# A decoder block of attention, linear attention and SwiGLU on one core: weight sums on VectorE, six early blocks, form loads on GpSimd's queue

## The chip, the core and the metric

One core of a Trainium2 chip runs the whole kernel in one launch. The metric is the device time of one execution in microseconds (us). The kernel before takes 2258.38 us (median of 3 runs, 2248.99 to 2261.52). Engines: TensorE (PE; PEld are its weight loads), VectorE (DVE), ScalarE (ACT), GpSimd (POOL) and SyncE (SP), which here only issues transfers. GpSimd issues transfers too, in the same queue as its own operations.

## The reference

One block of a transformer with 512 tokens and 2048 features, in float32. The first half mixes tokens by eight heads of softmax attention with low-rank queries and keys, and by four heads of gated linear attention (GLA); the second is a gated feed-forward network (FFN) of width 5632. Each half is normed before and after, and modulated by columns worked out from a vector `c`.

```python
ada = jax.nn.silu(c) @ w_ada[l] + b_ada[l]
shift_m, scale_m, gate_m, shift_f, scale_f, gate_f = [
    t[:, None, :] for t in jnp.split(ada, N_MOD, axis=-1)]
h = rms_norm(x, g_pre_mix[l]) * (1.0 + scale_m) + shift_m
z = h @ w_in[l]
...
o = jnp.concatenate([o_mla, o_gla], axis=-1) @ w_out[l]
x = x + gate_m * rms_norm(o, g_post_mix[l])
h = rms_norm(x, g_pre_ffn[l]) * (1.0 + scale_f) + shift_f
f = (jax.nn.silu(h @ w_ffn_gate[l]) * (h @ w_ffn_up[l])) @ w_ffn_down[l]
x = x + gate_f * rms_norm(f, g_post_ffn[l])
```

## The kernel before

A float32 product is made of three products of halves: each operand is split into a high part (a cast to a narrower format on ScalarE) and a low part (a subtraction on VectorE), and `mm3` (L213) multiplies high by high, high by low and low by high (L214 to L216). Weights arrive by SyncE's queue in pieces of 1 MB (a `wr` tile, four buffers) and are split by `load_split` (L203 is the low part) or, in the FFN, by `wparts` (L904 high, L905 low, into eight `wh` buffers).

The program is written down in an order, and a scheduler with a cost table of its own then sets the order of each engine's instructions; within an engine they run in that order. Small activations are `t2` tiles of 128 by 512, 73 in all.

Ahead of the FFN: `ada` (L228) makes one modulation column from a 1 MB weight piece by a product and a sum on VectorE. 96 columns are needed; the last 64 come from the generator `more`, a few at each step of the fillers, which are pieces of projection work (`fill_qk`, `fill_vr`, `fill_out`) that stand between the attention's steps. `lowrank` (L429) norms the low-rank queries and keys at the same time as the first fillers run.

`out_group` makes the output projection (16 tiles of sums, multiplied by a gain on GpSimd, L887), and `second_norm` (L793) adds the residual, norms each token tile, and multiplies it into `y` (L811, VectorE), which TensorE transposes (L814) and ScalarE scales into `h2` (L820).

The FFN multiplies in seven products in place of eight (the Winograd form of Strassen's scheme). Its activation operands are the forms a11, a12, a22 and s1 to s4, made by `first_forms` (from the first two token tiles) and `more_forms` (needing all four); `parts` splits them (L831 high, L832 low), `minus` is L836. Its weight operands are sums of the four quarters of the weights, made one into the next. `vadd` (L925) adds on VectorE, `padd` (L922) on GpSimd.

There are 22 blocks of 256 columns. The products q1 and q2 need only a11 and a12 and plain weights; for the first `PRO` = 2 blocks they are made early, among the steps of the second norm (the generator `norms`, moved on by `advance`), so that those blocks have five products left in the up loop and the other 20 have seven. Each product of the up loop is two times 24 `mm3`-parts of 256 columns. The results q1 and sg (a silu of a sum of q1 and q2) of an early block stay in `t2` tiles. After every second block `pair_forms` makes the seven forms of the result for the down loop, splits them and stores them to device memory (`spill_parts`, L949, GpSimd's queue). The down loop (five column groups `c_`, two halves `p` each) takes the forms back with `back` (L1025, SyncE's queue), makes seven products a half, and adds each to an accumulator on VectorE. The last two blocks are multiplied plainly at the end: `gate_rows` (L256, L257, L260) fetches gain rows through GpSimd's queue, `gl` fetches the last spilled tiles, the low parts of the last weights are made on GpSimd (L1084), and each sum is added (L1099), squared (L1101) and multiplied by its gain (L1102, GpSimd) before the closing norm.

## Time and profile before

| What | Value |
|---|---|
| Median of 3 runs | 2258.38 us |
| The profiled execution | 2255.43 us |
| Its span on the core | 2253.7 us |
| TensorE busy | 2109.3 us, 94% |
| VectorE busy | 1764.0 us, 78% |
| ScalarE busy | 907.7 us, 40% |
| GpSimd busy | 540.4 us, 24% |
| Mean granted TensorE clock | 0.972 |

Busy time adds up what an engine spends on instructions, with the time that an instruction stands for access to memory within it. TensorE's clock is granted at 2.4 GHz (1.0) or at 1.2 (0.5); a stretch's figure is the mean. A wait is put down to the instruction that released it last. The stages by time: up to 575 us the projections and both kinds of attention, to 767 the output projection, to 900 the second norm with the early blocks, to 1756 the up loop, to 2184.8 the down loop, then the last two blocks and the closing norm.

### The profile page before, as it was taken

To read this page: it belongs to the slowest core of one execution; us is meant where nothing else is said; L and a number is where in the kernel's file an instruction comes from. 1 tells how busy PE (TensorE), PEld (TensorE's weight loads), DVE (VectorE), ACT (ScalarE), POOL (GpSimd) and SP (SyncE) were. 2 spreads that over 40 slices of the span, in tenths; PEclk is the share of its full clock that TensorE was granted. 3 is DMA by queue.
4 is the path that set the end of the run, shared out by engine and by line. 5 is a ranking of instruction groups with operands and counts; after the bars stand their busy time and mean duration, and the time that the engine had idled before them with its cause. 6 is when DMAs were issued, how large, how long until landed. Compare 5 with 4: busy or idle time off the path is not lost. (4 is left out here: it accounts for less than half of the span.)

```text
span 2253.7 us, 32197 instructions
## 1 busy us (share of the span) xinstructions
PE 2109.3 (94%) x12714; PEld 1851.7 (82%) x12714; DVE 1764.0 (78%) x2095; ACT 907.7 (40%) x1265; POOL 540.4 (24%) x436
## 2 busy tenths in 40 slices
PE   7999999996999967999999999999999799999977
PEld 5888777773888867999999999999999687777866
DVE  6885787886475778888888888887887669888984
ACT  5433222324233664444434434434444353333332
POOL 0000000000212332323333333333332232131136
PEclk9999999996999979999999999999999999999989
DMA  8882586885575742434434424433433647564334
GB/s 333 317 306 100 210 306 246 316 311 199 187 247 202 260 178 75 178 133 158 160 122 149 173 113 146 178 113 141 178 128 125 244 178 273 213 217 148 128 131 150
DMA packets 91578, 432.18 MB, mean 192 GB/s; under 512 B 12168, under 2 KB 12280, under 8 KB 54817
## 3 DMA queue, kind: packets, MB, share of 16 engines
q1 hardware_dynamic: 69840, 360.09, 44.0%
q0 software_dynamic: 21584, 70.02, 8.1%
q8 instruction: 100, 1.64, 0.3%
q14 instruction: 52, 0.43, 0.1%
q10 hardware_dynamic: 2, 0.01, 0.0%
HBM read 370.80 MB, written 59.26 MB: 191 GB/s over the span
## 5 line engine op out<-in xcount | busy, mean ns | idle before, releaser
L905 DVE TENSOR_TENSOR wh<-wr,wh 128x1024 fp32r<-128x1024 f32 x448 | 677.8, 1524 | 214.7 <-ACT wh L904 210.3
L904 ACT CAST wh<-wr 128x1024 fp32r<-128x1024 f32 x448 | 464.6, 1050 | 649.0 <-PE ps L215 247.1
L214 PE MATMUL ps<-t,wh 128*128 128x256 f32 x2464 | 705.1, 286 | 18.8 <-ACT wh L904 9.0
L216 PE MATMUL ps<-t,wh 128*128 128x256 f32 x2464 | 704.9, 286 | 12.1 <-DVE wh L905 11.9
L215 PE MATMUL ps<-t,wh 128*128 128x256 f32 x2464 | 703.6, 286 | 4.4 <-DVE t L832 4.4
L214 PEld LDWEIGHTS ps<-t,wh 128*128 128x128 f32 x2464 | 479.0, 194 | 22.5 <-ACT wh L904 11.4
L216 PEld LDWEIGHTS ps<-t,wh 128*128 128x128 f32 x2464 | 478.7, 194 | 15.5 <-DVE wh L905 15.2
L215 PEld LDWEIGHTS ps<-t,wh 128*128 128x128 f32 x2464 | 479.0, 194 | 5.8 <-DVE t L832 5.7
L922 POOL TENSOR_TENSOR wr<-wr 128x1024 f32<-128x1024 f32 x88 | 223.5, 2540 | 500.5 <-DVE wh L905 232.1
L228 DVE CUSTOM_DVE_ANT_0 wr<-wr,cB 128x2048 f32<-128x2048 f32 x96 | 219.2, 2285 | 41.1 <-DMA wr<-w_ada 41.0
L215 PE MATMUL ps<-wh,t 128*128 128x512 f32 x560 | 222.9, 398 | 22.1 <-DVE wh L905 22.1
L214 PE MATMUL ps<-wh,t 128*128 128x512 f32 x560 | 221.4, 396 | 11.4 <-DMA t<-gd 11.3
L216 PE MATMUL ps<-wh,t 128*128 128x512 f32 x560 | 219.9, 395 | 0.5 <-DMA t<-gd 0.5
L202 ACT CAST hi<-wr 128x1024 fp32r<-128x1024 f32 (+3 forms) x122 | 122.7, 1010 | 223.1 <-PE ps L215 134.1
L203 DVE TENSOR_TENSOR lo<-wr,hi 128x1024 fp32r<-128x1024 f32 (+3 forms) x122 | 145.1, 1193 | 67.0 <-ACT hi L202 66.5
L215 PE MATMUL ps<-t,hi 128*128 128x512 f32 x432 | 173.0, 400 | 3.1 <-DVE t L302 3.0
L922 POOL TENSOR_TENSOR wr<-wr,wr 128x2048 f32<-128x2048 f32 x20 | 102.6, 5129 | 303.1 <-DVE wh L905 198.7
L216 PE MATMUL ps<-t,lo 128*128 128x512 f32 x432 | 170.4, 395 | 0.0
L214 PE MATMUL ps<-t,hi 128*128 128x512 f32 x432 | 168.7, 398 | 1.3 <-ACT t L300 1.3
L214 PE MATMUL ps<-hi,t 128*128 128x512 f32 x400 | 161.4, 404 | 1.0 <-DVE t L209 0.9
L925 DVE TENSOR_TENSOR wr<-wr,wr 128x1024 f32<-128x1024 f32 (+1 forms) x108 | 153.3, 1420 | 5.5 <-DMA wr<-w_fu 3.2
L215 PE MATMUL ps<-lo,t 128*128 128x512 f32 x400 | 156.6, 392 | 0.3 <-DVE lo L203 0.3
(230 smaller groups left out, 2656.6 us busy)
## 6 DMA issues: line engine op xcount, KB each, us to landing
wr<-w_ada SPq DMA_DIRECT2D x96, 1024.0 KB, 5.8
wr<-w_fg SPq DMA_DIRECT2D x48, 1024.0 KB, 5.0
wr<-w_fu SPq DMA_DIRECT2D x44, 1024.0 KB, 7.2
wr<-w_fd SPq DMA_DIRECT2D x40, 1024.0 KB, 4.9
gd<-t POOLq DMA_DIRECT2D x148, 256.0 KB, 2.6
t<-gd SPq DMA_DIRECT2D x148, 256.0 KB, 5.3
wr<-w_kqvr SPq DMA_DIRECT2D x24, 1024.0 KB, 4.9
wr<-w_out SPq DMA_DIRECT2D x22, 1024.0 KB, 5.5
```

Of the source, the lines that this page charges most:

```text
L202: A.copy(out=hi[:, :n], in_=r)
L203: V.tensor_tensor(out=lo[:, :n], in0=r, in1=hi[:, :n], op=ALU.subtract)
L214: T.matmul(ps, lhsT=a, rhs=c_, start=start, stop=False)
L215: T.matmul(ps, lhsT=a, rhs=d_, start=False, stop=False)
L216: T.matmul(ps, lhsT=b, rhs=c_, start=False, stop=stop)
L228: V.tensor_tensor_reduce(out=raw, in0=raw, in1=cB, scale=1.0, scalar=0.0, op0=ALU.mult, op1=ALU.add, accum_out=adac[:, j:j + 1])
L904: A.copy(out=hi, in_=src)
L905: V.tensor_tensor(out=lo, in0=src, in1=hi, op=ALU.subtract)
L922: nc.gpsimd.tensor_tensor(out=out, in0=a, in1=b, op=ALU.add)
L925: V.tensor_tensor(out=out, in0=a, in1=b, op=ALU.add)
```

## The change

- Every sum of FFN weights is made by `vadd` on VectorE; `padd` is gone. The gain products L887 and L1102 and the low parts L1084 go from GpSimd to VectorE as well, and `y` (L811) from VectorE to ScalarE.
- `PRO` is 6: six blocks have q1 and q2 made beside the second norm, and `advance` moves it two steps on after each half product, in all of them.
- Sixteen modulation columns go into `fill_qk`, four before each of its four pieces; `fill_vr` has three instead of four at each of 12 steps, and `fill_out` one or two instead of two. They are 64 as before.
- `back` loads spilled forms by GpSimd's queue.

```diff
--- before.py
+++ after.py
@@ -28,7 +28,7 @@
 MAGIC = 12582912.0
 N_T2 = 73
 NBLK = DFF // 256
-PRO = 2
+PRO = 6
 ATT_SCALE = 192.0 ** -0.5
 GLA_SCALE = 128.0 ** -0.5
 
@@ -454,6 +454,8 @@
             pss = [bank("A") for _ in range(4)]
             for kq in (2, 3):
                 w = load_split(w_kqvr[half, kq], 4, 512)
+                for _ in range(4):
+                    next(more)
                 for k, b in ORDER[kq == 3]:
                     mm3(pss[b], cut(w[k], b * P, P), hT[4 * kq + k], kq + k == 2, kq + k == 6)
                 if kq == 3:
@@ -467,7 +469,7 @@
             k0 = 2 if ci < 2 else 0
             for kq in range(k0, 4):
                 w = load_split(w_kqvr[2 + ci, kq], 4, 512)
-                for _ in range(4):
+                for _ in range(3):
                     next(more)
                 for k, b in ORDER[kq == 3]:
                     first, last = kq == k0 and k == 0, kq + k == 6
@@ -499,7 +501,7 @@
             w = ahead
             if i < 7:
                 ahead = load_split(w_out[todo[i + 1]], 4, 512)
-            for _ in range(2):
+            for _ in range(1 + q):
                 next(more)
             if q == 0:
                 pss = [bank("A") for _ in range(NT)]
@@ -808,7 +810,7 @@
         yield
         for n in range(4):
             y = t2()
-            V.tensor_scalar(y, og[t][n], v2, None, op0=ALU.mult)
+            A.activation(y, og[t][n], AF.Copy, scale=v2)
             ps = bank("B")
             for k in range(4):
                 T.transpose(ps[:, k * P:(k + 1) * P], y[:, k * P:(k + 1) * P], ident)
@@ -884,7 +886,7 @@
             o = og[t][n] = fetch(og[t][n])
             V.tensor_tensor(out=o, in0=pss[t], in1=o, op=ALU.add)
             A.activation(pss[t], o, AF.Square, accum_out=osum[:, 4 * t + n:4 * t + n + 1])
-            nc.gpsimd.tensor_tensor(out=o, in0=o, in1=ggm[n], op=ALU.mult)
+            V.tensor_tensor(out=o, in0=o, in1=ggm[n], op=ALU.mult)
 
     for n in range(1):
         out_group(n, range(NT))
@@ -918,9 +920,6 @@
                 mm3(ps[:, b * 256:(b + 1) * 256], cut(w, kk * 256 + b * P, P), rh,
                     first and kk + b == 0, last and kk + b == 4)
 
-    def padd(out, a, b):
-        nc.gpsimd.tensor_tensor(out=out, in0=a, in1=b, op=ALU.add)
-
     def vadd(out, a, b):
         V.tensor_tensor(out=out, in0=a, in1=b, op=ALU.add)
 
@@ -932,7 +931,7 @@
             ps = bank("A")
             for s in range(2):
                 up_product(ps, wparts(raws[s][:, o:o + 1024]), f, s, s == 0, s == 1)
-                advance(2 if j == 0 else 3)
+                advance(2)
             if f == "a11":
                 A.copy(out=q1, in_=ps)
         vadd(sg, ps, q1)
@@ -990,7 +989,7 @@
             else:
                 q1, sg = early[j]
             vadd(b11, b11, b12)
-            padd(b12, b12, b22)
+            vadd(b12, b12, b22)
             product("q5", "s1", b11, "A")
             product("r7", "s3", b12, "A")
             vadd(b11, b11, b22)
@@ -1001,7 +1000,7 @@
                 vadd(w_, pss["r7"], q1)
                 vadd(q1, pss["q5"], q1)
                 vadd(c22, pss["q5"], w_)
-            padd(b11, b11, b21)
+            vadd(b11, b11, b21)
             product("q4", "a22", b11, "B")
             if s == 1:
                 minus(w_, pss["q4"], w_)
@@ -1022,7 +1021,7 @@
 
     def back(d):
         t = t2(F32R)
-        dma(out=t.bitcast(F32), in_=d)
+        dma2(out=t.bitcast(F32), in_=d)
         return t
 
     acc = [[{} for _ in range(2)] for _ in range(2)]
@@ -1049,8 +1048,8 @@
             product("q1", "a11", b11)
             b22, b12 = raw_of(w_fd[c_, 1, 2 * p + 1]), raw_of(w_fd[c_, 0, 2 * p + 1])
             product("q2", "a12", b21)
-            padd(b11, b11, b12)
-            padd(b12, b12, b22)
+            vadd(b11, b11, b12)
+            vadd(b12, b12, b22)
             product("r3", "s4", b22)
             product("q5", "s1", b11)
             product("r7", "s3", b12)
@@ -1081,7 +1080,7 @@
             hi, lo = t2(F32R), t2(F32R)
             r = raw[:, k * 512:(k + 1) * 512]
             A.copy(out=hi, in_=r)
-            nc.gpsimd.tensor_tensor(out=lo, in0=r, in1=hi, op=ALU.subtract)
+            minus(lo, r, hi)
             row.append((hi, lo))
         wl.append(row)
     fsum = cp.tile([P, 4 * NT + 1], F32, name="fsum")
@@ -1099,7 +1098,7 @@
             V.tensor_tensor(out=f, in0=ps, in1=f, op=ALU.add)
             sq = t2()[:, 0:w]
             A.activation(sq, f, AF.Square, accum_out=fsum[:, 4 * t + j:4 * t + j + 1])
-            nc.gpsimd.tensor_tensor(out=f, in0=f, in1=ggf[n][:, o:o + w], op=ALU.mult)
+            V.tensor_tensor(out=f, in0=f, in1=ggf[n][:, o:o + w], op=ALU.mult)
         v = small(1, "v1")
         V.tensor_reduce(out=v, in_=fsum[:, 4 * t:4 * t + len(parts_)], axis=AX.X, op=ALU.add)
         v = rsqrt(v, D)
```

The scheduler orders the instructions anew. On VectorE in the second norm, before: the last forms (L832), the sum `sg` of the second early block (`t_6304`, out of the bank `ps_6449`), then the first results of block 0.

```order
L832 TENSOR_TENSOR t_6497<-t_6204,t_6496 128x512
L832 TENSOR_TENSOR t_6502<-t_5739,t_6501 128x512
L832 TENSOR_TENSOR t_6534<-t_6207,t_6533 128x512
L905 TENSOR_TENSOR wh_6827<-wr_6699,wh_6826 128x1024
L832 TENSOR_TENSOR t_6539<-t_5742,t_6538 128x512
L925 TENSOR_TENSOR t_6304<-ps_6449,t_6303 128x512
L836 TENSOR_TENSOR t_6032<-ps_6609,t_6032 128x512
L905 TENSOR_TENSOR wh_6864<-wr_6856,wh_6863 128x1024
```


VectorE at the same place, after (`minus` is L838 there, the low part L834, `vadd` L924): `t_6304` stands among the low parts of the forms, and the sums of the third and fourth early block (`t_6531`, `t_6672`) follow it.

```order
L834 TENSOR_TENSOR t_6516<-t_6164,t_6515 128x512
L834 TENSOR_TENSOR t_6521<-t_5729,t_6520 128x512
L924 TENSOR_TENSOR t_6304<-ps_6417,t_6303 128x512
L834 TENSOR_TENSOR t_6562<-t_6204,t_6561 128x512
L834 TENSOR_TENSOR t_6567<-t_5739,t_6566 128x512
L834 TENSOR_TENSOR t_6571<-t_6207,t_6570 128x512
L834 TENSOR_TENSOR t_6576<-t_5742,t_6575 128x512
L924 TENSOR_TENSOR t_6531<-ps_6608,t_6530 128x512
L907 TENSOR_TENSOR wh_6856<-wr_6790,wh_6855 128x1024
L924 TENSOR_TENSOR t_6672<-ps_6731,t_6671 128x512
```


The sum of the second early block stands before the last four low parts now, and behind it come early blocks in place of block 0.

GpSimd's queue at a pair boundary of the up loop, before: the spills of a pair's forms (L949) with a weight sum (L922) among them.

```order
L949 DMA gd_9032<-t_9028 128x512
L949 DMA gd_9026<-t_9021 128x512
L949 DMA gd_9034<-t_9029 128x512
L949 DMA gd_9041<-t_9037 128x512
L922 TENSOR_TENSOR wr_9072<-wr_9072 128x1024
L949 DMA gd_9043<-t_9038 128x512
L949 DMA gd_9050<-t_9046 128x512
```


VectorE at such a boundary, after: the forms (L834, L838), the splits (L907) and the weight sums (L924) of the next block.

```order
L834 TENSOR_TENSOR t_10916<-t_10253,t_10915 128x512
L907 TENSOR_TENSOR wh_11116<-wr_10934,wh_11115 128x1024
L834 TENSOR_TENSOR t_10925<-t_10684,t_10924 128x512
L907 TENSOR_TENSOR wh_11148<-wr_11143,wh_11147 128x1024
L907 TENSOR_TENSOR wh_11178<-wr_11143,wh_11177 128x1024
L924 TENSOR_TENSOR wr_11143<-wr_11143,wr_11145 128x1024
L924 TENSOR_TENSOR wr_11145<-wr_11145 128x1024
L907 TENSOR_TENSOR wh_11211<-wr_11143,wh_11210 128x1024
L907 TENSOR_TENSOR wh_11239<-wr_11145,wh_11238 128x1024
L924 TENSOR_TENSOR wr_11143<-wr_11143,wr_11145 128x1024
L924 TENSOR_TENSOR t_11205<-ps_10965,t_11175 128x512
L907 TENSOR_TENSOR wh_11268<-wr_11143,wh_11267 128x1024
```


The sums of the weights stand between VectorE's splits, and none is left on GpSimd.

SyncE's queue at the start of the down loop, before: form loads (L1025) with weight loads (L910) among them.

```order
L1025 DMA t_16522<-gd_7224 128x512
L1025 DMA t_16524<-gd_7226 128x512
L1025 DMA t_16526<-gd_8146 128x512
L1025 DMA t_16528<-gd_8148 128x512
L910 DMA wr_16754<-w_fd 128x2048
L1025 DMA t_16568<-gd_7197 128x512
L1025 DMA t_16570<-gd_7199 128x512
L1025 DMA t_16572<-gd_8119 128x512
```


GpSimd's queue there, after: the last spills (L948) and the first form loads (L1024).

```order
L948 DMA gd_16432<-t_16428 128x512
L948 DMA gd_16426<-t_16421 128x512
L1024 DMA t_16440<-gd_7664 128x512
L948 DMA gd_16434<-t_16429 128x512
L1024 DMA t_16442<-gd_7666 128x512
L1024 DMA t_16444<-gd_8348 128x512
L1024 DMA t_16446<-gd_8350 128x512
L1024 DMA t_16490<-gd_7672 128x512
L1024 DMA t_16492<-gd_7674 128x512
L1024 DMA t_16494<-gd_8356 128x512
L1024 DMA t_16496<-gd_8358 128x512
```


The loads have moved from among the weight loads to behind the spills of the last forms; the second load stands behind the last spill. In the same way the last eight loads (`gl`) stand behind L257 and L260 on GpSimd's queue at the end of the down loop.

## Rows read from the trace of the kernel before

**Rows 1.** page, part 1: busy us of each engine (share of the span) xinstructions

```profile
PE 2109.3 (94%) x12714; PEld 1851.7 (82%) x12714; DVE 1764.0 (78%) x2095; ACT 907.7 (40%) x1265; POOL 540.4 (24%) x436
```

**Rows 2.** busy time by stage: window, length, engines' busy us, PEclk, DMA share, GB/s

```profile
500.00:575.00 75.00, 52.14 (x184) 33.09 (x184) 44.92 (x85) 33.83 (x56) 10.79 (x21) 0.73 0.55 201
767.00:900.00 133.00, 103.24 (x665) 93.14 (x664) 106.78 (x161) 80.56 (x167) 38.95 (x31) 0.88 0.44 162
900.00:1756.00 856.00, 839.65 (x6887) 835.10 (x6888) 710.76 (x666) 366.42 (x420) 280.66 (x222) 0.99 0.40 148
1756.00:1821.00 65.00, 50.55 (x203) 39.72 (x201) 39.42 (x25) 27.38 (x37) 22.68 (x12) 0.92 0.51 197
1821.00:2184.80 363.80, 344.21 (x1485) 280.71 (x1483) 320.88 (x278) 140.49 (x149) 83.02 (x17) 0.99 0.53 189
2184.80:2253.70 68.90, 49.07 (x204) 36.99 (x203) 29.98 (x62) 13.68 (x39) 42.95 (x38) 0.89 0.40 147
```

**Rows 3.** waits of TensorE, 767 to 900 us: us in total, times, longest us

```profile
PE ps L814 <- DVE t L811: 10.4, 5, 3.8
```

**Rows 4.** groups by form: line, engine, operation, shapes, count | busy us, mean ns

```profile
L905 DVE TENSOR_TENSOR wh<-wr,wh 128x1024 fp32r<-128x1024 f32 x448 | 677.8, 1524 | 214.7 <-ACT wh L904 210.3 <-DMA t<-gd 1.5
...
L922 POOL TENSOR_TENSOR wr<-wr 128x1024 f32<-128x1024 f32 x88 | 223.5, 2540 | 500.5 <-DVE wh L905 232.1 <-DVE wr L925 175.2 <-issue 93.0
...
L228 DVE CUSTOM_DVE_ANT_0 wr<-wr,cB 128x2048 f32<-128x2048 f32 x96 | 219.2, 2285 | 41.1 <-DMA wr<-w_ada 41.0
...
L925 DVE TENSOR_TENSOR wr<-wr,wr 128x1024 f32<-128x1024 f32 x88 | 107.5, 1222 | 4.9 <-DMA wr<-w_fu 3.2
...
L925 DVE TENSOR_TENSOR wr<-wr,wr 128x2048 f32<-128x2048 f32 x20 | 45.8, 2291 | 0.6
```

**Rows 5.** timeline, GpSimd and VectorE, 1012 to 1030 us: start us, us, operation

```profile
1015.48 2.50 POOL L922 TENSOR_TENSOR wr<-wr 128x1024 f32<-128x1024 f32 x1
...
1015.63 3.62 DVE L836 TENSOR_TENSOR t<-t,t 128x512 f32<-128x512 f32 x2
...
1023.90 2.35 DVE L905 TENSOR_TENSOR wh<-wr,wh 128x1024 fp32r<-128x1024 f32 x2
```

**Rows 6.** busy time of a stretch within full up blocks

```profile
1640.00:1680.00 40.00, 40.00 (x334) 39.94 (x334) 32.48 (x30) 16.90 (x21) 13.18 (x9) 1.00 0.35 130
```

**Rows 7.** timeline, GpSimd and VectorE, 1891 to 1903 us (down loop)

```profile
1891.31 10.16 POOL L922 TENSOR_TENSOR wr<-wr,wr 128x2048 f32<-128x2048 f32 x2 [30.34 <-DMA wr<-w_fd]
...
1893.00 4.01 DVE L905 TENSOR_TENSOR wh<-wr,wh 128x1024 fp32r<-128x1024 f32 x1 [1.53 <-DMA t<-gd]
...
1897.54 5.01 DVE L905 TENSOR_TENSOR wh<-wr,wh 128x1024 fp32r<-128x1024 f32 x1
```

**Rows 8.** waits of TensorE, 1821 to 2184.8 us

```profile
PE ps L215 <- DVE wh L905: 19.6, 10, 3.8
```

**Rows 9.** busy time of a stretch at half clock in the second norm

```profile
825.60:849.50 23.90, 11.48 (x48) 10.01 (x49) 19.49 (x27) 16.04 (x36) 7.78 (x3) 0.50 0.28 105
```

**Rows 10.** DMA issues: what, queue, count, KB each, median us from issue to landing

```profile
t<-gd SPq DMA_DIRECT2D x148, 256.0 KB, 5.3
...
t<-og POOLq DMA_DIRECT2D x16, 256.0 KB, 5.5
```

**Rows 11.** waits of SyncE's queue, 1700 to 1821 us

```profile
SPq L910 <- DVE wr L925: 30.6, 2, 18.8
```

**Rows 12.** timeline of the end, 2180 to 2216 us

```profile
2180.17 1.28 DVE L925 TENSOR_TENSOR t<-t,t 128x512 f32<-128x512 f32 x2
...
2187.47 0.51 POOL L257 DMA_DIRECT2D gg<-t  x1 [31.50 <-DVE t L256]
...
2189.62 2.17 POOL L260 DMA_DIRECT2D t<-gg  x4 [1.64 <-issue]
...
2191.80 19.85 POOL L1084 TENSOR_TENSOR t<-wr,t 128x512 fp32r<-128x512 f32 x16
```

**Rows 13.** waits of TensorE, 2184.8 to 2253.7 us

```profile
PE ps L215 <- POOL t L1084: 11.4, 12, 8.3
```

## The prediction

> **What bounds the kernel now.** I read the page's first part, then the busy time by stage. TensorE is busy 2109.3 of the 2253.7 us of the span [rows 1]; the stages show where it is not [rows 2]. Six stretches hold nearly all that can be won: the tail of the attention (500 to 575 us: 22.9 idle), the second norm (767 to 900: 29.8), the up loop (900 to 1756: 16.4 over ten pairs of blocks), the start of the down loop (1756 to 1821: 14.5), its rest (19.6) and the end (19.8, of which 11.4 waits for GpSimd [rows 13] and 8.4 is the chain behind the last product). A low clock comes on top: over 133 us at a mean granted clock of 0.88, 16 us of full-speed time are lost, idle time included.
>
> What releases TensorE differs. In the second norm it is mostly VectorE and the casts behind it [rows 3]. In the two loops it is VectorE's low parts (L905), though VectorE has idle time in both. The groups say why: L905 takes 1524 ns on average, and an addition of the same size (L925) takes 1222 [rows 4]. The timeline shows the difference: a pair of subtractions that should take about 1.3 us takes 3.62 while GpSimd's addition L922 runs for 2.50 [rows 5], and in the down loop a split takes 4.01 and 5.01 beside two GpSimd additions of 10.16 together [rows 7]. So VectorE stands while GpSimd adds.
>
> **Sums of weights on VectorE (up loop).** 88 additions leave GpSimd (2540 ns each) for VectorE (1222) [rows 4]. Ends overlap: of two 1024-column operations in 2.35 us [rows 5] the second starts 1.14 after the first, of two 512-column ones in 1.28 [rows 12] some 0.61 after. For a pair of full blocks VectorE then needs 28 splits and 16 sums x 1.14, and 18 results and 11 forms x 0.61: 50.2 + 17.7 = 67.9 us. TensorE needs 2 x 7 x 48 = 672 products of 256 columns at 40.00/334 = 0.120 us [rows 6], 80.5 us. VectorE has 12 us to spare, and nothing makes it stand. Today's ten pair boundaries cost 16.4 us, and the clock (0.99 over 856 us) up to 8.6. In the new order the tightest place, the forms of a pair among the next block's splits, still leaves some 1.7 us. I take **-18** (bounds -8 to -24).
>
> **The same in the down loop.** 20 additions of 2048 columns cost VectorE 2291 ns [rows 4]. For each half of a column group: 14 splits x 1.14 + 4 sums x 2.21 + 14 accumulations x 0.61 = 33.3 us, against 7 x 24 products of 512 columns at 0.23 (344.21 us for 1485 are 0.232, a little of it at half clock [rows 2]) = 38.6. Ten waits of 19.6 us [rows 8] lose their cause; the last group, with 14 more combining operations a half, keeps a few. With the clock **-16** (-8 to -22).
>
> **Six blocks beside the second norm.** Each early block brings 2 x 48 products, 11.5 us; six bring 69 where two brought 23. They cost nothing in themselves, since the blocks skip them later. Idle there is 29.8; one half-clock stretch of 23.9 us holds 11.48 of work [rows 9] and so loses 5.7, the shorter ones some 3.5: 39 us. In the new order, from token one's residual to the sum sg of the second early block, VectorE has 23 operations of 1024 columns, 63 of 512 and 30 tiny ones (0.1 by my estimate): 67.4 us without a stop. TensorE comes to the product whose bank that sum frees after 336 x 0.120 + 57 x 0.23 + 52 x 0.1 = 58.6. It stands 9 us, or up to 18 with the round trips of the two reciprocal roots, and 4 at half clock. 39 less 13 to 22 is **-20** (bounds -8 to -33). The 16 products y move to ScalarE, busy 80.56 of 133 us there [rows 2]: nothing, unless ScalarE is late, when the transposes wait for it as they now wait for L811 [rows 3].
>
> **The price of six.** Blocks 0 to 5 have five products left, 240 x 0.120 = 28.7 us. VectorE needs 18 x 1.14 + 8 x 0.61, and 3.3 for its share of the forms: 28.7. Both are full for six blocks. The early results also hold 12 tiles instead of 4, so that some 70 of 73 are taken, and the first pair's 14 spill tiles go through the few left: **+5** (0 to +15).
>
> **Spilled forms on GpSimd's queue.** A load there lands 5.5 us after issue, on SyncE's queue 5.3 [rows 10]: no price in itself. But the queue has an order. At the start of the down loop the loads stand behind the last spill, which waits for the last low part. After the last up product VectorE still has a result, a split, a product, two additions of 2.21 us and three small operations between: 9.8 us. Then the issue of the spill and 5.3 to 5.5 us to land: the second form tile is there about 15.7 us after the last up product. TensorE stands 16 and loses 2 at half clock, 18. Today the same stretch has 14.5 idle [rows 2], behind a form load that stands on SyncE's queue behind a weight load waiting for a buffer [rows 11], and by my estimate 4 at half clock. **0** (-4 to +5). At the end the loads of the last block stand behind L257 and four L260, today issued from 2187.47 to 2191.79 [rows 12]. Then two to eight issues of 0.54 and 5.5: the first product comes some 12.5 us after the down loop, today 8.3 [rows 13]. But the low parts no longer come at 1.24 us each from GpSimd (16 in 19.85 us, with 0.7 us of products for each), so the rest runs at TensorE's rate: 12.5 + 2 for the last loads + 2 at half clock + 192 x 0.23 = 60.7 against 68.9 - 8.4 = 60.5. **0** (-3 to +5).
>
> The Trainium skill speaks against this move: "SBUF — State Buffer", section "SBUF: two separate sides", says that a transfer issued by GpSimd has its descriptors written by GpSimd's own cores, which some VectorE operations lock out, 620 ns becoming about 3100, and advises SyncE's or ScalarE's queue. The same page ("Who interferes with whom") leaves out additions and subtractions of two tiles, nearly all that VectorE does in the down loop, and by that the trace's 5.5 us agrees; by the 3100 ns the sum would be some 2.5 us worse for each of ten exposed issues.
>
> **Columns in the first fillers.** Sixteen column sums (2285 ns each [rows 4], with 1 MB of loads) come before the low-rank norms, and 12 fewer in the next fillers, 4 fewer in the output projection. TensorE is full there, so a late split costs: 0 to +6. In the attention's tail three sums of 2.3 us instead of six stand among the operations that TensorE waits for, of 22.9 us idle: -2 to -8. **-3** (-8 to +6).
>
> **Sum.** -18 - 16 - 20 + 5 + 0 + 0 - 3 = -52. The profiled execution took 2255.43 us, 1.7 more than its span and 2.95 below the median 2258.38; 52 off gives 2203.4 and, against the median, **2206**.
>
> **Rivals.** (1) VectorE has no room where it is full: the second norm gives back only 8, six blocks cost 15 and the up loop 10 instead of 18 is won. Against the forecast 12 + 10 + 8 = 30: 2236. For it speaks that both engines need 28.7 us a block; against it that early blocks give VectorE a lead.
> (2) Slower: L905 does not get faster, because what stretches it to 1.52 us is something that stays, such as the transfers, and the additions come on top. The place is the six blocks: 10 x 0.30 us more on 28.7 is 3 a block, 18 in all, no boundary gains anything, and the second norm loses the 0.3 on some 30 splits. 2258 + 18 - 6 = 2270. It decides from L905 staying over about 1.4 us. The rows speak against it: the long ones lie beside GpSimd's additions alone [rows 5, 7].
> (3) Starved loads: each issue on GpSimd's queue waits out a VectorE operation of up to 2.29. 28 loads of 2.8 us are 79 for a group whose products last 76: 5 x 3, and ten exposed issues x 2.3 at the start and the end, with the steady gain kept: +38, 2244. Against it, L260's four issues at 0.54 [rows 12].
> (4) Better: the second norm loses most of its gaps (-33), the boundaries theirs (-24 and -20), the six blocks cost nothing: 13 + 6 + 4 + 5 = 28 better, 2178.
> (5) The columns hold up the low-rank norms: SyncE and VectorE are filled by 16 x 2.3 = 37 us before the fillers' splits, and a third shows: +15, 2221.
>
> **How the numbers follow.** Forecast 0.58 (its own bounds 2190 to 2222), (1) 0.16, (2) 0.05, (3) 0.04, (4) 0.08, (5) 0.09. Leaving out (2), (3), half of (4) and the far end of (1) gives the range 2183 to 2240. A measurement of this kernel tells some 0.5% (11 us) from no change: faster is all but (2), half of (3), and 0.05 for several mishaps at once: 0.88; within 0.5%: 0.07, with the mild half of these; slower: 0.05.
>
> **What would show it.** Right: L905 at about 1.22 us and no GpSimd sums; no idle time at the pair boundaries from 1020 us on; one gap of 14 to 18 us at the start of the down loop behind form loads on GpSimd's queue, and one of about 12 at the end; VectorE's busy time still near 1765 us, since 187 us of additions replace about 172 of standing. Wrong: long L905 beside transfers, gaps before the splits of blocks 0 to 5 of more than 15 us, or new gaps between 200 and 500 us.

## The result

The changed kernel takes 2199.97 us (median of 4 runs, 2194.42 to 2202.13), against 2259.72 for the kernel before in the same comparison: a ratio of 0.9741, with a 95% interval of 0.9706 to 0.9777, or some 59 us less. The prediction was 2206 with a range of 2183 to 2240, so the forecast and the size of the gain were right. In part that is luck: five of its terms were off by 5 to 19 us each, three too small and two too large, and these nearly cancelled. The profiled execution took 2194.42 us, with a span of 2192.6. Two executions of this study were slow and stand in no ratio: one of before + columns (2291.75 us), and one of the changed kernel with its forms by SyncE (4130.78 us), whose stages are read from a further execution.

The first part of the changed kernel's page (it answers to [rows 1]), and the groups of VectorE's splits and weight sums, by form (they answer to [rows 4]; busy us, mean ns, then the idle time before them):

```profile
PE 2078.5 (95%) x12714; PEld 1839.2 (84%) x12714; DVE 1754.2 (80%) x2236; ACT 919.3 (42%) x1277; POOL 227.7 (10%) x427
```

```profile
L907 DVE TENSOR_TENSOR wh<-wr,wh 128x1024 fp32r<-128x1024 f32 x448 | 540.9, 1220 | 157.1 <-ACT wh L906 153.8 <-PE ps L216 0.3
...
L924 DVE TENSOR_TENSOR wr<-wr,wr 128x1024 f32<-128x1024 f32 x88 | 107.3, 1221 | 3.6 <-DMA wr<-w_fu 2.2
L924 DVE TENSOR_TENSOR wr<-wr 128x1024 f32<-128x1024 f32 x88 | 106.9, 1221 | 1.5
L924 DVE TENSOR_TENSOR wr<-wr,wr 128x2048 f32<-128x2048 f32 x40 | 91.5, 2288 | 11.5 <-DMA wr<-w_fd 10.8
```

GpSimd's busy time falls by 313 us and VectorE's does not rise. The split takes 1220 ns in place of 1524: 448 x 0.304 = 136 us of standing are gone. That it stood for GpSimd can be read in the trace of the kernel before by itself: the 77 of its 448 splits that overlapped an operation of GpSimd on tiles took 2992 ns in the mean, and the other 371 took 1220, none of them over 1227. The 88 moved sums of 1024 columns and the 20 of 2048 cost 107 + 46 us.

The busy time by stage (window, length, then busy time of PE, PEld, DVE, ACT and POOL; the granted clock, the DMA share and GB/s stand last; it answers to [rows 2]):

```profile
499.20:558.40 59.20, 44.93 (x185) 30.18 (x184) 36.62 (x74) 26.74 (x50) 10.24 (x20) 0.83 0.46 173
732.50:1074.00 341.50, 306.05 (x2252) 292.12 (x2251) 270.30 (x345) 183.40 (x295) 27.55 (x51) 0.94 0.49 183
1074.00:1719.30 645.30, 645.26 (x5378) 645.05 (x5376) 555.51 (x585) 290.73 (x329) 60.57 (x112) 1.00 0.40 151
1719.30:2118.80 399.50, 383.99 (x1681) 316.39 (x1681) 335.91 (x320) 168.38 (x185) 78.60 (x147) 0.98 0.55 203
2118.80:2192.60 73.80, 46.74 (x206) 38.48 (x204) 47.94 (x96) 13.95 (x39) 6.94 (x13) 0.82 0.43 157
```

Over the last 16 blocks of the up loop TensorE is never idle and never at half clock. The windows end at the same product in each kernel, found by counting products in the trace: where 2149, 2332 and 3203 products outside the FFN's loops have gone ahead, the first product of block 6 (2016 up products stand before it in any order), the last up product, the gain rows' transpose that closes the down loop, and the end. The same cuts in every kernel of this study (lengths in us, from each one's profiled execution):

| Kernel | Ahead | Attention's tail | Output projection | Second norm to block 6 | Blocks 6 to 21 | Down loop | End | Sum |
|---|---|---|---|---|---|---|---|---|
| before | 500.1 | 75.0 | 174.9 | 337.9 | 668.5 | 427.9 | 69.3 | 2253.7 |
| changed | 499.2 | 59.2 | 174.1 | 341.5 | 645.3 | 399.5 | 73.9 | 2192.6 |
| changed, again | 504.6 | 66.1 | 174.2 | 337.9 | 645.3 | 400.1 | 74.2 | 2202.3 |
| before + sums | 503.6 | 72.3 | 174.1 | 326.2 | 645.3 | 398.5 | 69.9 | 2190.0 |
| before + columns | 505.1 | 59.3 | 174.2 | 337.5 | 668.5 | 426.9 | 69.5 | 2240.9 |
| before + logarithms last | 504.5 | 74.4 | 174.1 | 337.7 | 668.7 | 424.5 | 69.4 | 2253.2 |
| changed, two early blocks | 506.7 | 66.7 | 174.2 | 325.6 | 645.3 | 402.9 | 73.3 | 2194.6 |
| changed, y on VectorE | 501.1 | 66.2 | 174.2 | 334.3 | 645.3 | 401.2 | 73.7 | 2196.0 |
| the same, bank emptied by ScalarE | 503.1 | 62.2 | 174.2 | 328.6 | 645.3 | 402.4 | 73.5 | 2189.2 |
| changed, forms by SyncE | 505.4 | 62.9 | 174.1 | 335.6 | 645.3 | 398.7 | 59.1 | 2181.1 |
| first mix | 503.5 | 63.8 | 174.2 | 326.0 | 645.3 | 402.1 | 59.0 | 2174.0 |
| second mix | 506.9 | 59.8 | 174.2 | 323.1 | 645.3 | 390.2 | 59.5 | 2159.0 |

Two rows of one kernel show how far a cell can be trusted: the stretch ahead differs by 5.4 us, the attention's tail by 6.9 and the second norm by 3.6, with the same order of instructions; from the up loop on they agree within 0.6. The 6.9 of the tail are the granted clock: TensorE waits 14.3 us there in both, but is busy for 44.9 us at a mean clock of 0.83 in one and for 51.8 at 0.72 in the other. From before to the changed kernel: -0.9, -15.8, -0.8, +3.6, -23.2, -28.4 and +4.6.

### The profile page after: what moved, and what is told of

It reads as the page before. It is cut to its first block, busy times and chain, and to the rows that moved or that the text cites. A ratio compares the mean times of both kernels' runs of the same rounds, so it can differ in the third digit from the quotient of the medians.

```text
span 2192.6 us, 31994 instructions
## 1 busy us (share of the span) xinstructions
PE 2078.5 (95%) x12714; PEld 1839.2 (84%) x12714; DVE 1754.2 (80%) x2236; ACT 919.3 (42%) x1277; POOL 227.7 (10%) x427
## 5 line engine op out<-in xcount | busy, mean ns | idle before, releaser
L907 DVE TENSOR_TENSOR wh<-wr,wh 128x1024 fp32r<-128x1024 f32 x448 | 540.9, 1220 | 157.1 <-ACT wh L906 153.8
L214 PE MATMUL ps<-wh,t 128*128 128x512 f32 x560 | 218.5, 391 | 10.8 <-DMA t<-gd 10.8
L215 PE MATMUL ps<-wh,t 128*128 128x512 f32 x560 | 218.9, 391 | 2.9 <-DVE wh L907 2.9
L216 PE MATMUL ps<-wh,t 128*128 128x512 f32 x560 | 217.5, 390 | 1.8 <-DMA t<-gd 1.8
L924 DVE TENSOR_TENSOR wr<-wr,wr 128x1024 f32<-128x1024 f32 (+1 forms) x128 | 198.9, 1554 | 15.1 <-DMA wr<-w_fd 10.8
L948 POOL DMA_DIRECT2D gd<-t x148 | 80.0, 542 | 837.7 <-ACT t L833 785.9
L924 DVE TENSOR_TENSOR t<-ps,t 128x512 f32<-128x512 f32 x222 | 149.7, 683 | 9.2 <-issue 8.0
```

Of the source, the lines that this page charges most:

```text
L214: T.matmul(ps, lhsT=a, rhs=c_, start=start, stop=False)
L215: T.matmul(ps, lhsT=a, rhs=d_, start=False, stop=False)
L216: T.matmul(ps, lhsT=b, rhs=c_, start=False, stop=stop)
L907: V.tensor_tensor(out=lo, in0=src, in1=hi, op=ALU.subtract)
L924: V.tensor_tensor(out=out, in0=a, in1=b, op=ALU.add)
L948: dma2(out=d, in_=v.bitcast(F32))
```

## The experiments

Ratios are to the kernel before, timed beside it on the same chip, with 95% intervals.

**One part alone: the sums.**

```diff
     def padd(out, a, b):
-        nc.gpsimd.tensor_tensor(out=out, in0=a, in1=b, op=ALU.add)
+        V.tensor_tensor(out=out, in0=a, in1=b, op=ALU.add)
```

> The kernel before with only the weight sums on VectorE: nothing else of the change. By the stages of the traces: up loop from block 6 on 668.5 to about 645 us (-23), the stage from the second norm to block 6 337.9 to 320 to 330 (-8 to -18), the down loop 427.9 to 400 to 415 (-13 to -28), the end unchanged. Theory 'the sums are the change': 45 to 65 us faster than before. Rival 'the parts need each other' (the queue move in the down loop above all): under 40 us faster.

Measured: 2193.95 us, a ratio of 0.9724 (0.9705 to 0.9743), 63.6 us faster than before: as much as the whole change. A split takes 1224 ns. By stage -11.7 in the second norm, -23.2 in the up loop, -29.4 in the down loop. This is the first theory, and the rival falls: the down loop fills without the move to GpSimd's queue. TensorE's waits from the end of the up loop on (us in total, times, longest us):

```profile
PE ps L215 <- POOL t L1084: 12.1, 13, 8.9
PE ps L214 <- DMA t<-gd: 10.6, 2, 6.0
PE ps L215 <- DVE wh L905: 3.0, 2, 2.0
```

The waits for L905 are down to two, in the last column group, from the ten of [rows 8]. So all the other parts of the change together are worth about nothing (its ratio and that of the changed kernel timed beside it, 0.9742, have overlapping intervals), and the rest of the study asks which of them give and which take.

**One part alone: the columns.**

```diff
                 w = load_split(w_kqvr[half, kq], 4, 512)
+                for _ in range(4):
+                    next(more)
...
-                for _ in range(4):
+                for _ in range(3):
                     next(more)
...
-            for _ in range(2):
+            for _ in range(1 + q):
                 next(more)
```

> The kernel before with the columns alone moved (16 in the first fillers, 3 and 1 or 2 later). In the changed kernel the matmuls outside the FFN run 17.5 us earlier from the attention's tail on. If the columns do that, by themselves or by the order that they cause, this kernel is 15 to 20 us faster than before, with the attention's tail as in the changed kernel (one wait of about 10 us for L683's tile, none of 7 for the reciprocal). If the tail's gain needs another part of the change: within 5 us of before.

Measured: 2245.47 us, a ratio of 0.9934 (0.9907 to 0.9960), about 15 us faster (13 by the medians), at the lower end of the first theory's 15 to 20 or just under it. The difference lies in the attention's tail (75.0 to 59.3). Part of such a figure is the clock, which varies from execution to execution; over the table's rows the three tails without the moved columns take 72.3 to 75.0 and the nine with them 59.2 to 66.7, 11 us less in the mean. So the part gives some four times the 3 us that I had put on it.

**A rival for the tail's gain.** With the columns moved the scheduler also put ScalarE's four logarithms behind its four exponentials; before, they alternate, with a table load between.

```diff
-        for e in gexp:
-            A.activation(e, e, AF.Exp)
-        for e in gexp:
-            A.activation(e, e, AF.Ln, bias=one_b)
+        ex = [A.activation(e, e, AF.Exp) for e in gexp]
+        for e in gexp:
+            i = A.activation(e, e, AF.Ln, bias=one_b)
+            for p_ in ex:
+                tc.add_manual_dep(i.ins, p_.ins.name, mybir.DependencyInfo(
+                    mybir.DependencyClass.NoSync, mybir.DependencyReason.DATA), reason="ln last")
```

> The kernel before, with only this added: ScalarE's four logarithms of the gates come after all four exponentials, as they stand in the changed kernel; the columns stay where they were. In before they alternate, and ScalarE loads a table seven times around them at 1.28 us each. Theory 'chain': the alternation holds up VectorE's gate operations and the scores behind them, so this kernel gains most of the 17.5 us: 12 to 18 us faster than before. Theory 'columns': what was won is that three column sums instead of six stand in VectorE's way; then only table loads are saved, off the path: 0 to 5 us faster.

Measured: 2262.97 us, a ratio of 1.0018 (1.0001 to 1.0035); the tail stays at 74.4. The grouping gives nothing, so the gain comes with the columns. TensorE's waits from 500 to 580 us, first with the logarithms last, then with the columns moved:

```profile
PE ps L605 <- DVE t L683: 8.9, 1, 8.9
PE ps L598 <- DVE rc L587: 6.1, 1, 6.1
PE ps L605 <- ACT t L600: 3.8, 3, 1.9
PE ps L624 <- DMA t<-wg: 2.5, 1, 2.5
```

```profile
PE ps L607 <- DVE t L683: 9.9, 1, 9.9
PE ps L607 <- ACT t L602: 2.8, 3, 1.5
PE ps L600 <- ACT t L587: 1.3, 1, 1.3
PE ps L600 <- DVE rc L589: 0.2, 1, 0.2
```

The wait for the reciprocal is what goes. VectorE's timeline in the kernel before shows what stood ahead of that reciprocal and of its scaling (L587, L588):

```profile
538.09 2.29 DVE L228 CUSTOM_DVE_ANT_0 wr<-wr,cB 128x2048 f32<-128x2048 f32 x1 [1.62 <-DMA wr<-w_ada]
...
541.37 0.16 DVE L587 RECIPROCAL rc<-sum 128x1 f32<-128x1 f32 x1
541.79 2.29 DVE L228 CUSTOM_DVE_ANT_0 wr<-wr,cB 128x2048 f32<-128x2048 f32 x1 [0.27 <-DMA wr<-w_ada]
...
544.01 0.28 DVE L588 TENSOR_SCALAR t<-t,rc 128x128 f32<-128x128 f32 x1
```

Two column sums, and VectorE waiting in its queue for their weights to land (1.62 and 0.27 us), with attention's small operations behind. I had priced a column in the tail at its 2.3 us; its price is that, the wait for its weights, and the low clock that follows the gap.

**Six early blocks.**

```diff
-PRO = 6
+PRO = 2
...
-                advance(2)
+                advance(2 if j == 0 else 3)
```

> The changed kernel with two early blocks instead of six, and the steps of the norm as before. Theory 'six cover nothing': the second norm has 30 us of idle time in both kernels because VectorE and ScalarE, not a lack of products, end it; this kernel is within 5 us of the changed one (55 to 65 faster than before). Rival 'six cover 20': without them TensorE idles 15 to 25 us more in the second norm, and the kernel is 12 to 25 us slower than the changed one (35 to 48 faster than before).

Measured: 2188.57 us, a ratio of 0.9691 (0.9662 to 0.9721). The intervals of this and of the changed kernel (0.9741, 0.9706 to 0.9777) overlap, but the stage does not leave a doubt: second norm to block 6 falls to 325.6, from 341.5 and 337.9 in the two executions of the changed kernel and 335.6 in the kernel with its forms by SyncE, which has the same second norm; the other kernels with two early blocks and the sums on VectorE take 323.1 to 326.2. Both theories expected the six blocks to give something or nothing; they cost 10 to 16 us. TensorE's waits from 740 to 910 us, in the changed kernel and with two early blocks:

```profile
PE ps L816 <- ACT t L813: 9.3, 5, 3.4
PE ps L214 <- DVE t L924: 8.3, 1, 8.3
PE ps L214 <- ACT t L936: 7.5, 2, 5.5
PE ps L214 <- ACT ps L888: 4.1, 3, 1.7
```

```profile
PE ps L816 <- ACT t L813: 17.6, 6, 5.2
PE ps L214 <- ACT ps L888: 3.0, 2, 2.1
PE ps L214 <- ACT wh L906: 2.8, 3, 1.8
PE ps L216 <- DVE wh L907: 1.6, 1, 1.6
```

The early products do cover 8 us of the transposes' wait for y. But they bring two waits of their own, for the banks of the first products (a bank holds a product's sums until another engine has read them), which ScalarE (L936, the copy of q1) and VectorE (L924, the sum sg) free late: 15.8 us. The wait for sg is the one that was worked out ahead, 9 us, measured 8.3. The five-product blocks add some 5 us of small gaps after 960 us, and TensorE's busy time in the stage is 7 us longer (306.05 against 298.97) at a lower mean clock (0.94 against 0.96).

**Is it the order on VectorE?** In two steps: y back on VectorE, then ScalarE in place of VectorE as the one who empties the bank of sg.

```diff
-            A.activation(y, og[t][n], AF.Copy, scale=v2)
+            V.tensor_scalar(y, og[t][n], v2, None, op0=ALU.mult)
```

> The changed kernel with the 16 products y of the second norm on VectorE again. Theory 'ScalarE late': TensorE's transposes wait 9.3 us for y and the early products 7.5 us for a bank that ScalarE empties late; without y ScalarE has 10 us less to do there, and the kernel is 6 to 12 us faster than the changed one (66 to 72 faster than before). Rival 'VectorE late': the sum sg that TensorE waits 8.3 us for comes 16 x 0.61 = 10 us later; the kernel is 0 to 10 us slower than the changed one (50 to 60 faster than before).

Measured: 2193.53 us, a ratio of 0.9709 (0.9683 to 0.9735); 65 us faster than before and just short of the first theory's 66 to 72; the stage takes 334.3 against 341.5, 337.9 and 335.6. ScalarE was late for y: the wait of the transposes falls from 9.3 to 3.7, and the wait for sg stays at 8.5. How much of it reaches the time is not settled: the median is some 5 us lower, within the intervals, and the stage says 1 to 7. With two early blocks the same move changes the stage little (325.6 with y on ScalarE; 326.0 and 323.1 in the mixed kernels below, with y on VectorE), though the transposes' wait falls there too, from 17.6 to 12.5 and 10.1.

```diff
-        vadd(sg, ps, q1)
+        A.copy(out=sg, in_=ps)
+        vadd(sg, sg, q1)
```

> The changed kernel with y on VectorE, and with the bank of an early block's second product emptied by ScalarE into sg, so that TensorE no longer needs VectorE's sum to go on. It is to be held against the kernel with y on VectorE alone (334.3 us from the second norm to block 6, one wait of 8.5 us for that sum). Theory 'order on VectorE': the wait for the sum, which stands behind the forms, is what six early blocks cost there; it goes, and the stage takes 324 to 329 us. Rival 'the work is only moved': VectorE's forms and splits are late anyway, TensorE waits as long for the next split or form, and the stage takes 331 to 337 us.

Measured: 2192.02 us, a ratio of 0.9702 (0.9678 to 0.9726); the stage takes 328.6, inside the first theory's 324 to 329. TensorE's waits there (740 to 910 us):

```profile
PE ps L214 <- ACT t L937: 5.1, 1, 5.1
PE ps L816 <- DVE t L813: 4.8, 4, 1.7
PE ps L214 <- ACT t L936: 4.4, 2, 2.4
```

The wait is not gone, it has moved to ScalarE's copy (L937) and is 3.4 us shorter, and the bank wait L936 shortened too. The stage is 5.7 us shorter, and TensorE's idle time in it falls by as much (30.2 to 24.5). That the position of the bank's release among the forms is worth about 6 us, near half of the six blocks' cost, is likely but not shown: the medians of the two kernels differ by less than 2 us, and three executions of one second norm lie 6 us apart. The stage still is 3 to 6 us above that with two.

**The queue of the form loads.** All of them on SyncE's queue again.

```diff
     def back(d):
         t = t2(F32R)
-        dma2(out=t.bitcast(F32), in_=d)
+        dma(out=t.bitcast(F32), in_=d)
         return t
```

> The changed kernel with all spilled forms fetched by SyncE's queue again. Theory 'the queue move costs at the end': there the first load landed 9.9 us after its issue because the four gain rows were moved ahead of it in the same queue; without that the end stage falls from 73.9 us to 60 to 66. At the start of the down loop the gap of 10.8 + 1.8 us behind the last spill is replaced by one behind weight loads, 6 to 14 us as before, and the loads among the weight loads cost 0 to 10 us more in the rest of the loop. In all 0 to 10 us faster than the changed kernel. Rival 'the move is what keeps the down loop full': over 10 us more in the down loop, and the kernel is slower than the changed one.

> One look at the changed kernel with all spilled forms fetched by SyncE's queue, for its stages (timed before: 14 us faster than the changed kernel). If the end made the difference, its last stage is 58 to 62 us in place of 73.9, and the down loop with its start is within 4 us of the changed kernel's 400; if the down loop did, the last stage is over 68.

Measured: 2184.45 us, a ratio of 0.9676 (0.9659 to 0.9693), 14 us faster than the changed kernel beside it, more than the 0 to 10 expected. The stages are those of the further execution (2182.84 us): the end takes 59.1 in place of 73.9, below the expected 60 to 66, and the down loop 398.7 against 399.5. The gain is the end, as expected, and nothing else. The mark beside them was the changed kernel itself:

> The changed kernel itself, beside the others of this call: 55 to 65 us faster than before. It is the mark for the three below.

It measured 2198.3 us, a ratio of 0.9742 (0.9720 to 0.9765).

The timeline of the changed kernel at the end of the down loop (2118.8 us) shows why:

```profile
2122.33 0.51 POOL L257 DMA_DIRECT2D gg<-t  x1 [104.27 <-DVE t L256]
...
2124.45 0.56 POOL L260 DMA_DIRECT2D t<-gg  x1 [1.61 <-issue]
2124.47 2.74 SPq L1089 DMA_DIRECT2D wr<-x1d  x2
2125.57 1.60 POOL L260 DMA_DIRECT2D t<-gg  x3 [0.55 <-issue]
2127.15 2.12 POOL L1024 DMA_DIRECT2D t<-gd  x4
...
2137.19 0.77 PE L214 MATMUL ps<-t,t 128*128 128x512 f32 x1 [18.17 <-DMA t<-gd]
```

The first load is issued 8.3 us after the last down product, much as worked out ahead (its issue at 7 to 8). But TensorE gets it 10.0 us after the issue, not 5.5: four gain rows had been put into the same queue just ahead, and the loads land behind them. The rows themselves took 6.8 to 9.8 us, where they took 3.5 to 4.3 before. Beside them, SyncE's queue had just issued two pieces of x1d of 1 MB each (L1089), and the DMA engines were all but full from 2128 to 2140 us (busy share 0.99 or more). With the forms by SyncE the rows again take 6.8 to 8.9 us beside x1d, without a form load behind them, but the form loads have been issued before all that and land after 5.1 to 5.7. How much of the 10.0 us is the order in the queue and how much the x1d beside it, no run separates.

**A version to beat both.** The changed kernel with two early blocks, y on VectorE (both as above), and a second `back` that uses SyncE's queue:

```diff
+    def back_sp(d):
+        t = t2(F32R)
+        dma(out=t.bitcast(F32), in_=d)
+        return t
...
-                    fs[f] = [[back(d) for d in gd[2 * c_ + q][f]] for q in range(2)]
+                    fs[f] = [[(back_sp if c_ == 0 else back)(d) for d in gd[2 * c_ + q][f]] for q in range(2)]
...
-    gl = [[[back(d) for d in v] for v in blk] for blk in gd[-1]]
+    gl = [[[back_sp(d) for d in v] for v in blk] for blk in gd[-1]]
```

> A version meant to be faster than both: the changed kernel with two early blocks, y on VectorE, and the forms of the first column group and of the last blocks fetched by SyncE's queue (the other groups stay on GpSimd's). If the six early blocks and ScalarE's y give nothing and GpSimd's queue costs at its two ends: the second norm to block 6 takes 315 to 326 us, the start of the down loop 0 to 10 less, the end 60 to 66: 15 to 35 us faster than the changed kernel. Rival 'VectorE late': y on VectorE costs 5 to 10 in the second norm, and the start of the down loop gains nothing: 5 to 12 us faster.

Measured: 2171.11 us, a ratio of 0.9621 (0.9607 to 0.9635), 27 us faster than the changed kernel beside it. The end takes 59.0. The start of the down loop gained nothing: TensorE's waits for form loads are 14.5 us there (10.8 + 1.8 in the changed kernel), and their place has moved from the first product to the fourth and sixth (counted in the trace, where 72 and 120 of the loop's `mm3`-parts, 24 to a product, stand before them). So the first group's loads were split between the queues:

```diff
-                    fs[f] = [[(back_sp if c_ == 0 else back)(d) for d in gd[2 * c_ + q][f]] for q in range(2)]
+                    get = back_sp if c_ == 0 and f in ("a11", "a12") else back
+                    fs[f] = [[get(d) for d in gd[2 * c_ + q][f]] for q in range(2)]
```

> As the mixed version before (2171 us), but of the first column group only the first two products' forms come by SyncE's queue, the rest by GpSimd's. There TensorE waited 9.9 and 4.6 us for the third and fifth product's forms, whose loads stood on SyncE's queue behind weight loads that wait for buffers. If the queue's order is the cause, the loads now go out some 10 us after the last up product and land by 15: the waits fall to 2 to 6 us, and the kernel is 6 to 14 us faster than the mixed version (94 to 100 faster than before). Rival 'the transfers themselves are the limit there': the waits stay over 10 us in sum, and it is within 4 us of the mixed version.

Measured: 2157.77 us, a ratio of 0.9549 (0.9526 to 0.9571), 101 us faster than before and some 13 faster than the first mix. TensorE's waits from the end of the up loop on, first mix and second:

```profile
PE ps L214 <- DMA t<-gd: 14.5, 2, 9.9
PE ps L215 <- DVE t L838: 3.4, 1, 3.4
PE ps L215 <- DVE wh L907: 2.9, 2, 1.9
```

```profile
PE ps L215 <- DVE t L838: 3.4, 1, 3.4
PE ps L214 <- DMA t<-gd: 3.3, 1, 3.3
PE ps L215 <- DVE wh L907: 3.0, 2, 2.0
```

The first two products' forms leave SyncE's queue before the loop begins, and those of the third leave GpSimd's queue right behind the last spill, while the first two products run. No run with one queue alone has both: on GpSimd's the first forms stand behind the last spill, on SyncE's the later ones behind weight loads that wait for a buffer.

## Why the prediction was right, step by step

**VectorE stood while GpSimd added: right.** L907 takes 1220 ns where 1.22 us was forecast, and the sums alone give 63.6 us. In the kernel before only the splits that overlap GpSimd's operations are long (2992 ns against 1220). The Trainium skill ("SBUF — State Buffer", section "SBUF: two separate sides") says that of a VectorE operation with two SBUF inputs and a GpSimd operation that reads SBUF, the one that starts first holds a shared pair of ports for its whole instruction, and the other is blocked. The trace agrees: in [rows 5] the pair of subtractions ends 1.27 us after the addition beside it does, about the 1.28 that such a pair takes by itself.

**The up loop: right in cause, small in size.** -18 was taken, with bounds of -8 and -24; it is -23.2 for 16 blocks, of which 12.7 was idle time and 10.5 the clock. The work count said VectorE needs 67.9 of 80.5 us, and no gap is left; I had taken 18 of the 16.4 + 8.6 us that the rows showed, and in these 16 blocks all of them went.

**The down loop: small in size.** -16 for the loop and 0 for its start; together -28.4. The loop lost all its waits but two (2.9 us of ten waits' 19.6). Behind its first 200 `mm3`-parts it takes 339.0 in place of 361.4, where 16 less was the sum. The start, up to there, takes 60.5 in place of 66.5, and the sums alone give 59.5: the 6 us are theirs, and I had left them out of the start; the queue's move gave nothing there, as forecast. The start was forecast as the same 18 us behind another cause. The cause came as described: the last spill is issued at 1729.24, 9.9 us after the last up product, where 9.8 was worked out. But the two loads that TensorE stood for, one just ahead of that spill and one just behind, landed after 3.0 and 3.7 us, not 5.3 to 5.5, so TensorE stood 10.8 + 1.8 us and not 16. GpSimd's timeline at the start of the down loop of the changed kernel (the first product's forms are loaded at L1024, the last low part is spilled at L948), and under it TensorE's first two waits for those forms:

```profile
1726.97 0.54 POOL L1024 DMA_DIRECT2D t<-gd  x1
1729.24 0.54 POOL L948 DMA_DIRECT2D gd<-t  x1 [1.73 <-DVE t L834]
1729.78 6.00 POOL L1024 DMA_DIRECT2D t<-gd  x11
...
1730.06 0.77 PE L214 MATMUL ps<-wh,t 128*128 128x512 f32 x1 [10.80 <-DMA t<-gd]
1733.51 0.80 PE L216 MATMUL ps<-wh,t 128*128 128x512 f32 x1 [1.83 <-DMA t<-gd]
```

**Six blocks beside the second norm: wrong.** -20 + 5 was the sum for the stage; it is -2 to +4, and of that the sums alone are -11.7, so the six blocks and y cost some 10 to 16. The step that failed is "39 less 13 to 22". (The operations counted for it add up to 67.7 us, not 67.4, which changes nothing.) It set the gaps of the kernel before, made partly by GpSimd's additions, against the one wait that I had worked out (8.3 us came for 9), as if the extra products filled all the rest. They filled about 8 us. What I left out is that each product needs a bank, that the bank is freed by an operation that stands on VectorE or ScalarE among the norm's own work, and that four more blocks bring 16 splits (two to a product), with as many casts, into just that stretch: a product is no filler where its operands and its bank come from the engines that are late.

**y on ScalarE at nothing: too low, by 1 to 7 us** in the changed kernel, which is not clear of the scatter; with two early blocks no cost shows in the stage. The cover that was named (ScalarE's idle time) was there on average: it was busy 106.77 of 155 us from 745 to 900. It was not there when the transposes asked. The wait that was named as the price of a lost cover is the one that came.

**The queue at the end: its cost too small.** 0, with +5 as the far end; +4.6 measured, as the sum of a gap of 18.2 us where 12.5 was worked out, and a faster rest. The failed step is "5.5 to land": it took the median of all such loads for one that stands behind four rows, with 2 MB of x1d moving beside them, and that took 10.0. As a part, the queue move at the end is worth +15 (73.9 against 59.1): without it the low parts that no longer come from GpSimd would have gained 10.

The Trainium skill's warning about transfers issued by GpSimd ("SBUF — State Buffer", section "SBUF: two separate sides") did not show: loads of forms land 4.8 us after issue in the median there, 5.3 on SyncE's queue before. What hurt at the end is what stood ahead of the loads and moved beside them.

**The columns: far too small.** -3 was taken, with bounds of -8 and +6; alone they give 13 to 15 (11 in the mean of the traces' tails). The step that failed priced three sums at their own duration. Nothing in the runs separates the sums from the changed order around them; only the grouped logarithms are excluded.

**The rivals.** None came whole. Of (1), that VectorE is full beside the second norm, its half on that stage is what happened, with ScalarE as a second cause; its half on the loops did not. Of (4), the loops did lose all their gaps (-23.2 and -28.4), and the second norm did not. (2), (3) and (5) are excluded by L907's 1220 ns, the 4.8 us of the loads and the unchanged 500 us ahead. The mechanism of the main term was right and carried the whole gain. That the number came out so near is luck: the gains that were too small (by 5, 12 and about 12 us) stand against a gain and a cost that were too favourable (by 13 to 19, and by 5).

## What to carry to other kernels

An addition on GpSimd beside a busy VectorE was paid for twice here: before giving work to the idle engine, compare the busy engine's mean duration for one form where the other runs and where it does not. More early work covers a chain of waits only if what frees its buffers and makes its operands is not on that chain's engines. A transfer's latency is that of its moment: look at what was put into its queue just ahead of it, at what the other queue moves beside it, and at which instruction the issuing engine must pass first, and split a burst between two queues when each is blocked at a different time.

## What the runs showed of the hardware

A VectorE subtraction of 128 by 1024 took 1220 ns, and 2992 in the mean where it overlapped an operation of GpSimd on tiles. With those gone, all 448 took 1206 to 1228 ns, beside transfers of up to 203 GB/s too (a mean over the down loop), so such transfers do not stretch it. Behind four broadcast rows in its queue, and with two 1 MB pieces moving from the other queue, a 256 KB load took 10.0 us in place of 3 to 5.5; the rows took 6.8 to 9.8 in place of 3.5 to 4.3. And TensorE can be kept without a gap and at the full granted clock for 645 us, 5378 recorded products, with VectorE busy 86% beside it.
